# Prompt attention's query, key and value loads in another layout, and a GpSimd power for linear attention's norm root

## The chip, the cores and the metric

The kernel runs on one core of one Trainium2 chip. The metric is the device time of one execution in microseconds. A core has five engines that run side by side, each with its own in-order instruction queue: TensorE (PE in the profile, with its weight loads as a row PEld of its own), VectorE (DVE), ScalarE (ACT), GpSimd (POOL) and SyncE (SP). SP, ACT and POOL also issue DMA transfers; all of these run on the core's 16 DMA engines. SBUF has 128 partitions; PSUM takes the results of TensorE.

## The reference

One layer of a decoder, for a prompt of 2048 tokens and for 8 samples of 8 new tokens each, width 1024, all in float32:

```python
xn = rmsnorm(x, g_pre_mix)
q_a, k_a, v_a, q_b, k_b, v_b, r_b, a_lr = split(xn @ w_in)
o_a = attn_fn(q_a, k_a, v_a)             # 8 heads of 64, three dilated windows, merged
o_b = gla_recurrent(q_b, k_b, v_b, logf) # 4 heads, linear attention in chunks
o_b = rmsnorm(o_b, g_gla_norm) * silu(r_b)
x = x + rmsnorm(concat(o_a, o_b) @ w_o, g_post_mix)
x = x + rmsnorm(conv_ffn(rmsnorm(x, g_pre_ffn)), g_post_ffn)
```

The three windows of the attention, the patterns, are (128 tokens, every token), (512, every 4th) and (2048, every 16th). Each pattern has its own softmax, and the outputs are merged with weights in proportion to the softmax denominators. The norm of `o_b` is a root mean square over the 128 values of each head.

## The kernel before

The kernel has three stages. The **sweeps** (`sweeps`, line 257) go over the tokens in four chunks of 512 (the last with the 64 sample tokens as well), twice: `sweep_b` (line 650) makes the projections of linear attention, `sweep_a` (line 408) those of softmax attention. Linear attention and the sample attention are generators that are advanced between the projections, so that their work goes in between TensorE's matmuls. Then comes **prompt attention** (`attention`, line 983), then the **tail** (`tail`, line 1297) with the output projection and the feed-forward part.

Products are made in float32 as split pairs: a matrix is cut into a high part that the fast matmul format holds and the rest, and three products (high by high, high by low, low by high) are added. For the scores of softmax attention two matmuls do: the contraction runs over 128 partitions, of which 64 hold the high part of a head's queries and 64 the low part, against keys whose high part (first matmul) or low part (second) stands twice, once for each half (`at_operands`, line 1094, and line 1856).

`sweep_a` writes to scratch memory in HBM, for each of the four pairs of heads (`pr`) and each chunk c, the high and low part of the queries (tensors `qh`, `ql`, lines 445 and 446) and of the keys (`kh`, `kl`, lines 425 and 426), each [4, 128, 512]: chunk, 64 values of each of the pair's two heads, token. The values go to the output `o_vp` (line 456), a row of 512 values per token.

`attention` goes over four pairs of heads, three patterns, four groups. `at_load` (line 1062) brings a pair's queries and keys to SBUF: for each head h a tile `aqs` with the queries' two parts, a tile `akh` with the keys' high part twice, a tile `akl` with the low part twice, each [128, 2048]. Each tile is filled by two transfers (z = 0, 1) of 64 partitions. For pair 0 the load is cut into the pieces (0,1), (1,2), (2,4) of chunks, the first of them issued from ACT near the end of the sweeps (`at_prefetch`, line 965); for the others the whole of it is issued on SP while the pair before is worked on, in two sets of buffers that alternate.

`at_loadv` (line 1078) brings the values of a group in four transfers of 64 KB: four blocks of 128 keys by 128 values (two heads), each row of 512 bytes. In the first two patterns each transfer fills one block, that is a quarter of the tile's columns on all 128 partitions; in the third pattern each fills 32 partitions over all columns. The call for group i + 2 stands in the program before group i; six buffers hold them.

A unit (`AtUnit`, line 1821) is a group's scores, softmax, transposes and product with the values, for two heads; the first two patterns have two units a group, the third has one. Scores run up to three units ahead of the product. The order of the units' matmuls on TensorE is tied down (`line` in `AtUnit`), and so is the order of POOL's work (`line`, line 1114): it gathers the queries of patterns two and three into dense tiles (`at_gather`, line 1121, tile `aqg`, five buffers), and does the merge of the pair before (`at_merge`, line 1130): the weights go through HBM (line 1195) and come back spread over 64 partitions (line 1183), then multiplications and additions follow (lines 1210, 1225 and 1235). The merge advances by one step per group. For pair 3 the merge runs at the end, in another form.

The norm of linear attention's output is `gla_norm` (line 794): ACT squares and sums the four heads of a block of 128 tokens, `rms_cols` (line 100) makes one over the root, and DVE multiplies (line 803). The result is transposed on TensorE (`gla_store`, line 807). It is called 17 times: for 16 blocks of the prompt and once for the samples. `rms_cols` has two forms. With "v" the root is found on DVE, by an estimate from the bits of the number and three Newton steps: ten small instructions. With "p" it is one GpSimd instruction, a power of -0.5; the four wide norms of the layer use this one (line 132).

All else is ordered by a planner, which puts each instruction on its engine's queue in the order of a simulated timeline.

Of the kernel before, what the change touches and what calls it, by code (L numbers as in the profile page):

```python
# [10 lines left out]
F32 = mybir.dt.float32  # L11
# [25 lines left out]
class Layer:  # L37
# [370 lines left out]
    def sweep_a(self, c):  # L408
        nc, a = self.nc, self.a
        xs = self.xnext  # L410
        u = 0
        for m in range(8):
            pr, isk = m // 2, m % 2
            wt = self.wget()
            for s0, n in self.subs(c):
                ps = self.psum.tile([128, 512], F32, name=self.n("pq"), tag="g1", bufs=3)
                self.gemm([(ps[:, :n], s0, n)], wt, xs, KT)
                npr = min(n, 512 - s0)
                if s0 == 0:
                    hi = self.st.tile([128, 512], F32R, name=self.n("qh"), tag="qh", bufs=2)  # L420
                    lo = self.st.tile([128, 512], F32R, name=self.n("ql"), tag="ql", bufs=2)
                src = ps[:, :npr]
                if isk:
                    self.split(hi[:, :npr], lo[:, :npr], src, "v")
                    nc.sync.dma_start(a["kh%d" % pr][c, :, s0:s0 + npr], hi[:, :npr].bitcast(F32))
                    nc.sync.dma_start(a["kl%d" % pr][c, :, s0:s0 + npr], lo[:, :npr].bitcast(F32))
                else:
                    rr = slice(s0 // 32, (s0 + npr) // 32)
                    hv, lv = (t.rearrange("p (i r) -> p r i", r=16)[:, rr, :] for t in (hi, lo))
                    sv = src.rearrange("p (r i) -> p r i", i=32)  # L430
                    nc.scalar.activation(hv, sv, AF.Copy, scale=-0.125)
                    nc.vector.scalar_tensor_tensor(lv, sv, -0.125, hv.bitcast(F32), op0=ALU.mult, op1=ALU.subtract)
                if isk:
                    kf = self.st.tile([128, 512], F32, name=self.n("kf"), tag="kf", bufs=2)
                    self.evac(kf[:, :n], ps[:, :n], "a")
                    nc.sync.dma_start(a["o_kp"][c, pr, :, s0:s0 + npr], kf[:, :npr])
                    if npr < n:
                        nc.sync.dma_start(a["o_ks"][pr], kf[:, npr:n])
                        nc.gpsimd.tensor_copy(self.ks[:, pr, :], kf[:, npr:n])
                elif npr < n:  # L440
                    qd = self.qbd[:, pr]
                    nc.vector.tensor_copy(qd[0:64, :, 0:8], ps[0:64, npr:n].rearrange("p (b t) -> p b t", b=8))
                    nc.vector.tensor_copy(qd[64:128, :, 8:16], ps[64:128, npr:n].rearrange("p (b t) -> p b t", b=8))
            if not isk:
                nc.sync.dma_start(a["qh%d" % pr][c], hi.bitcast(F32))
                nc.sync.dma_start(a["ql%d" % pr][c], lo.bitcast(F32))
            yield "q", m
        for nn in range(2):
            wv = [self.wget(), self.wget()]
            for t0, m in self.vblocks(c):  # L450
                ps = self.psum.tile([128, 512], F32, name=self.n("pv"), tag="g1", bufs=3)
                self.vgemm(ps, xs, t0, m, wv)
                vs = self.st.tile([128, 256], F32, name=self.n("vs"), tag="vs", bufs=self.AB["vsb"])
                self.evac(vs[:m], ps[:m, :256], "v")
                if m == 128:
                    (nc.gpsimd if c == 2 else nc.sync).dma_start(a["o_vp"][c * 512 + t0:c * 512 + t0 + 128, nn * 256:nn * 256 + 256], vs)
                else:
                    nc.sync.dma_start(a["o_vs"][:, nn * 256:nn * 256 + 256], vs[:64])
                yield "v", u
                u += 1  # L460
# [333 lines left out]
    def gla_norm(self, po, n, gb):  # L794
        nc, g = self.nc, self.gp
        ss = g.tile([128, 4], F32, name=self.n("gss"), tag="gss", bufs=2)
        junk = g.tile([128, 128], F32, name=self.n("gj"), tag="gj", bufs=self.SB["gj"])
        for h in range(4):
            nc.scalar.activation(junk[:n], po[:n, h, :], AF.Square, accum_out=ss[:n, h:h + 1])
        y = self.rms_cols(ss[:n], n, 1.0 / 128, 4, g, "gr")  # L800
        on = g.tile([128, 4, 128], F32, name=self.n("gon"), tag="gon", bufs=self.SB["gon"])
        for h in range(4):
            nc.vector.scalar_tensor_tensor(on[:n, h, :], po[:n, h, :], y[:n, h:h + 1],
                                           gb[:n, h * 128:h * 128 + 128], op0=ALU.mult, op1=ALU.mult)
        return on
# [256 lines left out]
    def at_load(self, pr, pieces=((0, 4),), qs="ss", to=None):  # L1062
        a, p = self.a, self.aq[pr % 2]
        QS, KH, KL = to or ([], [], [])
        for c0, c1 in pieces:
            for h in range(2):
                hs = slice(64 * h, 64 * h + 64)
                for L, nms in ((QS, ("ql", "qh") if h else ("qh", "ql")), (KH, ("kh", "kh")), (KL, ("kl", "kl"))):
                    nm = "qs" if L is QS else nms[0]
                    if not c0:  # L1070
                        L.append(p.tile([128, 2048], F32R, name=self.n("a" + nm), tag="a" + nm, bufs=self.AB["q"]))
                    t = L[h].rearrange("p (c j) -> p c j", c=4)
                    for z in range(2):
                        self.dq(qs[z]).dma_start(t[64 * z:64 * z + 64, c0:c1].bitcast(F32),
                                                 a["%s%d" % (nms[z], pr)][c0:c1, hs].rearrange("c p j -> p c j"))
                    yield QS, KH, KL

    def at_loadv(self, i):
        nc, e = self.nc, self.nc.gpsimd if i < 2 else self.nc.sync
        pr, pat, n = i // 12, i // 4 % 3, i % 4  # L1080
        es = slice(128 * pr, 128 * pr + 128)
        vo = self.a["o_vp"]
        t = self.aq[1].tile([128, 4, 128], F32, name=self.n("av"), tag="av", bufs=self.AB["v"])
        for j in range(4):
            if pat == 0:
                e.dma_start(t[:, j, :], vo.rearrange("(c r b i) e -> c b r i e", c=4, r=16, b=4)[n, j, :, :, es])
            elif pat == 1:
                e.dma_start(t[:, j, :], vo.rearrange("(c s r i) e -> r c s i e", c=4, s=4, r=4)[n, j, :, :, es])
            else:
                e.dma_start(t[32 * j:32 * j + 32],  # L1090
                                  vo.rearrange("(c r i) e -> c i r e", c=4, r=16)[j, :, 4 * n:4 * n + 4, es])
        self.vq += [t[:, j] for j in range(4)]
# [869 lines left out]
def pack_inputs(inp):  # L1962
# [14 lines left out]
    def vt(cols):  # L1977
# [27 lines left out]
    "o_y": (128, KT, T), "o_kp": (4, 4, 128, 512), "o_vp": (S, 512), "o_gp": (2, 128, 128), "o_cp": (128, NF, 2),  # L2005
    "o_ks": (4, 128, 64), "o_vs": (64, 512), "o_gs": (2, 128, 8, 128), "o_cs": (128, NF, 8, 2),
}
SCRATCH = {**{"%s%d" % (t, i): (4, 128, 512) for t in ("qh", "ql", "kh", "kl") for i in range(4)}, "awd": (3, 96, 128),
           "wbs": (12, 2, 128, 1024), "wst": (NF // 2, 2, 4, 128, 2, 512), "xst": (4, 14, 2, 128, 2 * H),
           "mixa": (128, 4, S), "mixb": (128, 4, T), "x1": (128, KT, T), "rs1": (128, T), "rs2": (128, T)}  # L2010

# [15 lines left out]
def build(nc, arrays, stages="saf", ext_scratch=()):  # L2027
# [5 lines left out]
    with tile.TileContext(nc, **TCK) as tc:  # L2033
        with tc.tile_pool(name="scratch", bufs=1, space=bass.MemoryType.DRAM) as dp:
            for n, s in SCRATCH.items():
                if n in ext_scratch:
# [15 lines left out]
```

## Time and profile before

| | |
|---|---|
| median of 3 runs | 2780.03 us (2777.55 to 2789.05) |
| the profiled execution | 2780.57 us, its span 2778.5 us |
| mean granted TensorE clock | 0.984 |
| sweeps | 0 to about 774 us |
| prompt attention | about 774 to 1086 us |
| tail | about 1086 to 2778 us |

The profile is of one execution. Times in it are microseconds, or nanoseconds where that is said; a line such as L1856 is the line of the kernel that issued the instruction. The busy time of an engine is the sum of its instructions; matmuls are pipelined, so a busy TensorE is not TensorE at its peak. The granted clock is TensorE's, 1.00 being full speed. The DMA share is the mean busy share of the 16 DMA engines in a stretch: 0.25 is four engines' worth; it can come out a little above 1. "A <- B" says that A waited for B. In the chain of waits the work that ended last is followed back from the end, each step to what released it.

### The profile page before, as it was taken

The numbers are of one execution on the slowest core, as the hardware profiler recorded it, in microseconds if no ns is written. First come the engines' busy times: TensorE is split into PE (matmuls) and PEld (weight loads), VectorE is DVE, ScalarE is ACT, GpSimd is POOL, SyncE is SP. The second block draws the span as 40 slices with busy tenths as digits, with TensorE's granted clock in tenths as the row PEclk, the third lists the DMA queues.
The fourth block names the chain that finished last, engine by engine and source line by source line (L and its number), as shares of the span: only waits on it lengthen the run. The fifth ranks groups of instructions, "written<-read, shape, count | busy, mean of one in ns | idle before, by whom it ended". The sixth has DMA issues, their size and how long they took to land.

```text
span 2778.5 us, 58351 instructions
## 1 busy us (share of the span) xinstructions
PE 2669.0 (96%) x22203; PEld 2530.5 (91%) x22203; DVE 1827.3 (66%) x4508; ACT 1271.4 (46%) x2961; POOL 568.2 (20%) x626
## 2 busy tenths in 40 slices
PE   7999999999989898999999999999999999999998
PEld 6888899888778787999999999999999999999997
DVE  7556555454347577467898889876576766666666
ACT  6535433333358686345554444543334433443332
POOL 4424242443323577002000020000020000200001
PEclk9999999999999899999999999999999999999998
DMA  8755446799798865368587688986698875976654
GB/s 319 245 183 194 154 134 204 270 326 367 267 209 173 186 157 147 106 214 305 177 288 288 223 292 291 360 298 227 211 344 283 293 235 199 332 253 212 221 187 154
DMA packets 286183, 661.67 MB, mean 238 GB/s; under 512 B 32128, under 2 KB 81920, under 8 KB 283856
## 3 DMA queue, kind: packets, MB, share of 16 engines
q1 hardware_dynamic: 255600, 579.53, 62.0%
q0 software_dynamic: 13216, 46.56, 5.2%
q10 hardware_dynamic: 17088, 31.86, 3.1%
q8 instruction: 175, 2.87, 0.4%
q14 instruction: 104, 0.85, 0.1%
HBM read 511.45 MB, written 146.37 MB: 237 GB/s over the span
## 4 chain that ended last, share of the span: by engine, by line
PE 78%; DMA 9%; DVE 6%; POOL 2%; issue 2%; ACT 2%; SPq 0%; ACTq 0%; DVEq 0%; POOLq 0%
PE pfd L92 17%; PE pv L399 9%; PE pfe L1624 8%; PE pfd L1624 8%; PE pfa L1624 8%; PE pbo L1427 7%; PE pq L92 6%; PE pfb L1624 4%; PE pas L1856 2%; DMA av<-out_o_vp 2%; DMA ws<-d_wst 2%; PE pao L1899 1%; PE pat L1882 1%; DMA raw<-in_xp 1%; DMA akl<-d_kl 1%
## 5 line engine op out<-in xcount | busy, mean ns | idle before, releaser
L70 ACT ACTIVATE ws<-wr 128x512 fp32r<-128x512 f32 (+1 forms) x482 | 292.8, 616 | 430.9 <-PE pfe L1624 137.6
L92 PE MATMUL pfd<-hh,ws 128*128 128x264 f32 x2816 | 475.4, 286 | 8.2 <-ACT ws L70 5.5
L92 PEld LDWEIGHTS pfd<-hh,ws 128*128 128x128 f32 x2816 | 400.9, 189 | 10.6 <-ACT ws L70 7.3
L73 DVE TENSOR_TENSOR ws<-wr,ws 128x512 fp32r<-128x512 f32 (+1 forms) x482 | 319.1, 668 | 117.7 <-ACT ws L70 112.5
L92 PE MATMUL pfd<-hl,ws 128*128 128x264 f32 x1408 | 302.2, 285 | 0.0
L1624 PE MATMUL pfe<-xh,ws 128*128 128x264 f32 x1496 | 291.5, 287 | 9.5 <-DVE u L1611 5.9
L1624 PE MATMUL pfa<-xh,ws 128*128 128x264 f32 x1496 | 290.0, 285 | 4.6 <-ACT ws L70 1.9
L1624 PE MATMUL pfd<-xh,ws 128*128 128x264 f32 x1408 | 290.8, 286 | 1.8 <-DMA ws<-d_wst 1.0
L1624 PEld LDWEIGHTS pfe<-xh,ws 128*128 128x128 f32 x1496 | 237.4, 190 | 11.3 <-DVE u L1611 7.0
L1624 PEld LDWEIGHTS pfa<-xh,ws 128*128 128x128 f32 x1496 | 235.3, 188 | 5.9 <-ACT ws L70 2.4
L399 PE MATMUL pv<-wh,xh 128*128 128x256 f32 (+1 forms) x816 | 234.2, 287 | 3.2 <-DVE th L696 3.2
L1624 PEld LDWEIGHTS pfd<-xh,ws 128*128 128x128 f32 x1408 | 232.5, 190 | 2.6 <-DVE ws L73 1.4
L399 PE MATMUL pv<-wh,xl 128*128 128x256 f32 (+1 forms) x816 | 232.3, 285 | 0.0
L399 PE MATMUL pv<-wl,xh 128*128 128x256 f32 (+1 forms) x816 | 231.9, 284 | 0.0
L92 PEld LDWEIGHTS pfd<-hl,ws 128*128 128x128 f32 x1408 | 225.8, 189 | 0.1
L1865 ACT ACTIVATE ass<-ass,aml 128x256 f32<-128x256 f32 (+1 forms) x384 | 173.6, 455 | 94.5 <-DVE aml L1861 68.8
L1624 PE MATMUL pfd<-xl,ws 128*128 128x264 f32 x704 | 201.2, 286 | 0.0
L1573 POOL DMA_DIRECT2D xl<-d_xst x52 | 28.2, 542 | 834.0 <-PE pfe L1624 495.7
L92 PE MATMUL pq<-xh,wh 128*128 128x512 f32 (+2 forms) x480 | 171.3, 366 | 10.3 <-ACT xh L234 7.8
L1624 PE MATMUL pfe<-xl,ws 128*128 128x264 f32 x616 | 176.3, 286 | 0.0
L1624 PE MATMUL pfa<-xl,ws 128*128 128x264 f32 x616 | 174.9, 284 | 0.0
L92 PE MATMUL pq<-xl,wh 128*128 128x512 f32 (+2 forms) x480 | 174.8, 365 | 0.0
(338 smaller groups left out, 6569.9 us busy)
## 6 DMA issues: line engine op xcount, KB each, us to landing
ws<-d_wst SPq DMA_DIRECT2D x248, 512.0 KB
wr<-in_wu SPq DMA_DIRECT2D x114, 512.0 KB
d_wst<-ws SPq DMA_DIRECT2D x88, 512.0 KB
wr<-in_wd SPq DMA_DIRECT2D x160, 256.0 KB
wr<-in_wt SPq DMA_DIRECT2D x60, 512.0 KB
wh<-d_wbs SPq DMA_DIRECT2D x35, 512.0 KB
wl<-d_wbs SPq DMA_DIRECT2D x35, 512.0 KB
skp<-in_ckt SPq DMA_DIRECT2D x16, 1024.0 KB
```

The source lines that it names most:

```text
L70: h = nc.scalar.activation(hi, src, AF.Copy)
L73: return h, (nc.gpsimd if lo_eng == "p" else nc.vector).tensor_tensor(lo, src, hi.bitcast(F32), op=ALU.subtract)
L92: mm = nc.tensor.matmul(o, ww[:, k, :], xx[:, s0:s0 + n], start=(k == order[0] and i == 0), stop=(k == order[-1] and i == 2))
L399: mm = nc.tensor.matmul(ps[:m, :256], x[:, t0:t0 + m], w[:, k % 4, :], start=(k == 0 and i == 0), stop=(k == KT - 1 and i == 2))
L1427: self.lastmm = nc.tensor.matmul(o, ww[:, k, :], xx[:, s0:s0 + n], start=k == self.WORD[0] and i == 0, stop=k == self.WORD[-1] and i == 2)
L1573: self.nc.gpsimd.dma_start(t.bitcast(F32), xo[i, z])
L1624: self.lastmm = nc.tensor.matmul(bank[:, :H], w[:, ww, k, :], xx, start=new and k == 0 and j == 0, stop=k == 3 and j == 2, skip_group_chec ...
L1856: self.line(nc.tensor.matmul(ps[:, sc:sc + nk], lq, rk[z], start=(z == 0), stop=(z == 1)))
L1865: ex = nc.scalar.activation(ssb[:, sc:sc + nk], ssb[:, sc:sc + nk], AF.Exp, bias=self.ml[:, idx, h:h + 1], scale=-1.0, accum_out=self.ml[: ...
L1882: self.line(nc.tensor.transpose(ptp[:, len(tl), :], ssb[:, sc + 128 * j:sc + 128 * j + 128], L.ident))
L1899: self.line(nc.tensor.matmul(po[64 * h:64 * h + 64, blk, :], L.vq[self.base + kb][:, 64 * h:64 * h + 64], pt[:, j, :], start=st, stop=sp))
```

## The change

Four edits:

- The queries' two parts go into one scratch tensor `qs` of [4, 128, 2, 512] instead of two of [4, 128, 512]. Each part is still one transfer of 256 KB.
- `at_load` fills a query tile with one transfer over 128 partitions, in which the high and the low part alternate from partition to partition (both heads have the same order). It fills a key tile with one transfer per chunk, over 128 partitions, in which a step of zero makes each row of the source go to two neighbouring partitions. A pair's load of four chunks has 2 query transfers instead of 4 and 16 key transfers instead of 8. The product sums over the partitions, so that only the order of the sum changes.
- `at_loadv` loads the second pattern as it does the third: a transfer fills 32 partitions over all columns.
- `gla_norm` asks for the "p" form of `rms_cols`.

```diff
@@ sweep_a @@
             if not isk:
-                nc.sync.dma_start(a["qh%d" % pr][c], hi.bitcast(F32))
-                nc.sync.dma_start(a["ql%d" % pr][c], lo.bitcast(F32))
+                for z, t in enumerate((hi, lo)):
+                    nc.sync.dma_start(a["qs%d" % pr][c, :, z], t.bitcast(F32))
@@ gla_norm @@
-        y = self.rms_cols(ss[:n], n, 1.0 / 128, 4, g, "gr")
+        y = self.rms_cols(ss[:n], n, 1.0 / 128, 4, g, "gr", "p")
@@ at_load @@
-                for L, nms in ((QS, ("ql", "qh") if h else ("qh", "ql")), (KH, ("kh", "kh")), (KL, ("kl", "kl"))):
-                    nm = "qs" if L is QS else nms[0]
+                for L, nm in ((QS, "qs"), (KH, "kh"), (KL, "kl")):
                     if not c0:
                         L.append(p.tile([128, 2048], F32R, name=self.n("a" + nm), tag="a" + nm, bufs=self.AB["q"]))
-                    t = L[h].rearrange("p (c j) -> p c j", c=4)
-                    for z in range(2):
-                        self.dq(qs[z]).dma_start(t[64 * z:64 * z + 64, c0:c1].bitcast(F32),
-                                                 a["%s%d" % (nms[z], pr)][c0:c1, hs].rearrange("c p j -> p c j"))
+                    t = L[h].rearrange("p (c j) -> p c j", c=4).bitcast(F32)
+                    src = a["%s%d" % (nm, pr)]
+                    if L is QS:
+                        self.dq(qs[0]).dma_start(t[:, c0:c1], src[c0:c1, hs].rearrange("c p z j -> (p z) c j"))
+                    else:
+                        for c in range(c0, c1):
+                            s = src[c, hs]
+                            self.dq(qs[c % 2]).dma_start(t[:, c], bass.AP(tensor=s.tensor, offset=s.offset,
+                                                                          ap=[s.ap[0], [0, 2], s.ap[1]]))
                     yield QS, KH, KL
@@ at_loadv @@
             elif pat == 1:
-                e.dma_start(t[:, j, :], vo.rearrange("(c s r i) e -> r c s i e", c=4, s=4, r=4)[n, j, :, :, es])
+                e.dma_start(t[32 * j:32 * j + 32], vo.rearrange("(c s r i) e -> r s i c e", c=4, s=4, r=4)[n, j, :, :, es])
```

More of the change, by code (lines that the diff above doesn't have):

```diff
@@ L2007 @@
 }
-SCRATCH = {**{"%s%d" % (t, i): (4, 128, 512) for t in ("qh", "ql", "kh", "kl") for i in range(4)}, "awd": (3, 96, 128),
+SCRATCH = {**{"%s%d" % (t, i): (4, 128, 512) for t in ("kh", "kl") for i in range(4)}, **{"qs%d" % i: (4, 128, 2, 512) for i in range(4)}, "awd": (3, 96, 128),
            "wbs": (12, 2, 128, 1024), "wst": (NF // 2, 2, 4, 128, 2, 512), "xst": (4, 14, 2, 128, 2 * H),
```

## The prediction

> **What bounds the kernel now.** I read the page's first and fourth part, then the windows, the chain of waits, and the timelines of one stage.
>
> ```profile
> span 2778.5 us, 58351 instructions
> ...
> PE 2669.0 (96%) x22203; PEld 2530.5 (91%) x22203; DVE 1827.3 (66%) x4508; ACT 1271.4 (46%) x2961; POOL 568.2 (20%) x626
> ...
> PE 78%; DMA 9%; DVE 6%; POOL 2%; issue 2%; ACT 2%; SPq 0%; ACTq 0%; DVEq 0%; POOLq 0%
> ```
>
> TensorE (PE) sets the pace, so only an edit that shortens PE's gaps can pay. The windows say where these are (columns: us, then busy time of PE, PEld, DVE, ACT, POOL, granted clock, DMA share, GB/s):
>
> ```profile
> 0.00:774.00 774.00, 744.85 (x6177) 648.41 (x6177) 410.60 (x1040) 326.42 (x736) 300.04 (x297) 0.99 0.69 243
> 774.00:1086.00 312.00, 274.95 (x2632) 241.63 (x2631) 209.18 (x960) 225.60 (x872) 171.22 (x179) 0.93 0.76 172
> ```
>
> Prompt attention, 774 to 1086, loses 37 us of PE and runs at a granted clock of 0.93 on the mean. It holds most of what the change touches. The chain of waits there shows its course (start us, us, what):
>
> ```profile
> 806.15 1.16 PE pas L1856 x8
> ...
> 809.20 1.13 PE pas L1856 x8
> ...
> 844.16 1.93 PE pas L1856 x16
> ...
> 874.76 17.07 DMA av<-out_o_vp
> ...
> 893.73 15.45 DMA av<-out_o_vp
> ...
> 927.98 1.10 PE pas L1856 x8
> ...
> 943.50 17.19 DMA av<-out_o_vp
> ...
> 1004.64 1.37 PE pas L1856 x8
> ...
> 1070.47 3.67 PE pas L1856 x16
> ```
>
> Four head pairs follow each other. The first score matmul of pair 0 starts here:
>
> ```profile
> L1856 PE MATMUL pas<-akh,aqs x128: 219/287/582, 773.5 to 1028.8; 128*128 128x256 f32 x120, 128*128 128x128 f32 x8
> ```
>
> "x8" are units of the first two patterns, "x16" those of the third. An undisturbed unit takes 809.20 - 806.15 = 3.05 us; from 809.20, the first unit of the second pattern, to the last unit at 844.16 and 3.7 for that unit it is 38.7 us. Eight units of the first pattern (24.4) and these give **63 us per pair** when PE never waits. The pairs really took 773.5 to 847.9 (74.4), to 927.98 (80.1), to 1004.64 (76.7) and to 1074.15 (69.5): together 300.7. PE's gaps inside them, in its weight-load timeline:
>
> ```profile
> 793.78 0.29 PEld L1856 LDWEIGHTS pas<-akh,aqs 128*128 128x128 f32 x1 [5.31 <-issue]
> 795.19 0.28 PEld L1856 LDWEIGHTS pas<-akl,aqs 128*128 128x128 f32 x1 [1.13 <-DMA akl<-d_kl]
> ...
> 891.87 0.20 PEld L1899 LDWEIGHTS pao<-apt,av 128*64 128x64 f32 x4 [3.70 <-DMA av<-out_o_vp]
> ...
> 905.65 0.42 PEld L1899 LDWEIGHTS pao<-apt,av 128*64 128x64 f32 x8 [4.35 <-DMA av<-out_o_vp]
> 909.23 0.30 PEld L1899 LDWEIGHTS pao<-apt,av 128*64 128x64 f32 x4 [3.16 <-DMA av<-out_o_vp]
> ...
> 960.73 1.15 PEld L1899 LDWEIGHTS pao<-apt,av 128*64 128x64 f32 x12 [8.29 <-DMA av<-out_o_vp]
> ```
>
> Transfers bound this stage, in two ways that the DMA windows keep apart (us, PE busy, clock, DMA share, GB/s):
>
> ```profile
> 418.00:420.00 2.00, 2.00 (x14) 0.99 1.05 404
> 420.00:422.00 2.00, 2.00 (x19) 1.00 1.03 387
> ```
> ```profile
> 889.00:890.00 1.00, 0.00 (x0) 1.00 0.25 67
> ```
> ```profile
> 944.00:946.00 2.00, 2.00 (x20) 1.00 1.07 208
> ```
> ```profile
> 911.00:914.00 3.00, 3.00 (x16) 0.50 0.66 186
> 986.00:989.00 3.00, 3.00 (x33) 1.00 1.04 174
> ...
> 1019.00:1022.00 3.00, 3.00 (x34) 1.00 0.27 82
> ```
>
> At 944 only query and key loads run, each on 64 partitions: all 16 DMA engines are busy and move 208 GB/s. At 418 256 KB transfers over 128 partitions run, with the same 2 KB rows: as busy, they move 390 to 404. At 889 and 1019 second-pattern value loads run alone: a share of 0.25 to 0.27, four engines of 16, and 67 to 82 GB/s. In line 1088 the outermost dimension of the source has size 4; in line 1090 (third pattern) it has 32, and at 986 these loads keep all engines busy at 174 GB/s, some of it other traffic. The row at 911 shows a restart after a gap: clock 0.50, and 16 matmuls where 33 run otherwise, so that some 2 us are lost behind each longer gap.
>
> **The change part by part.** *Query and key loads.* A pair moves 12 loads (line 1074) of 64 partitions by 8 KB, 6.29 MB. At 208 GB/s that is 30.2 us of all engines, at 390 it is 16.1. Eight 512 KB key loads become sixteen of 256 KB, four query loads two of 1 MB: six more issues a pair.
>
> ```profile
> L1074 SPq DMA_DIRECT2D akh<-d_kh x20: 444/606/2774, 759.2 to 934.9; - x20
> ```
> ```profile
> L1086 SPq DMA_DIRECT2D av<-out_o_vp x56: 536/595/1096, 774.6 to 1013.1; - x56
> ```
>
> At 0.6 us an issue this adds 3.6 us to SP's queue per pair, ahead of value loads; 18 such issues and 48 value issues of at most 0.6 make 40 of some 67 us, so SP's slack hides it; without that cover it would be 4 x 3.6 = 14 us. The rate after is bounded by 208 (no gain) and 404; I take 390, because the 418 row has the same rows and number of partitions.
>
> [...]
>
> *Second-pattern value loads.* The number of partitions of one DMA falls here, from 128 (one quarter of the columns) to 32 (all columns): the words "over all 128 partitions" don't fit, what changes is the outermost dimension, 4 to 32. Sixteen loads of 64 KB a pair cost 1.05 MB / 82 GB/s = 12.8 us on four engines. Bounds after: 1.05 / 174 = 6.0 us, and no gain. I take the 174 row, since line 1090 has the very form of the new line.
>
> [...]
>
> *What is late next.* With transfers early, PE waits for POOL, which gathers queries (L1126) between the pieces of the merge of the pair before, in one fixed order:
>
> ```profile
> 1028.37 0.53 POOL L1195 DMA_DIRECT2D d_awd<-awt  x1 [14.96 <-DVE awt L65]
> ...
> 1039.15 2.99 POOL L1225 TENSOR_TENSOR aop<-aop,awb 128x512 f32<-128x512 f32 x2 [2.08 <-DMA awb<-d_awd]
> ```
> ```profile
> 887.95 2.49 POOL L1225 TENSOR_TENSOR aop<-aop,awb 128x512 f32<-128x512 f32 x2 [8.78 <-DMA awb<-d_awd]
> ```
>
> Pair 3 shows a pair with little transfer trouble: its merge starts 1039.15 - 1004.64 = 34.5 us into the pair, the last gather frees PE at 1070.47, 31.3 later, and the unit takes 3.7. In pair 1 the start came 40 us in, because the weights landed 8.78 late. With transfers early I take 34.5 - 2.1 = 32.4 for pairs 1 to 3: 32.4 + 31.3 + 3.7 = **67.4 each**, 202.2 against 226.3: **-24.0**. Bounds: 64 each (63 and the merge's matmuls), -34; and no gain.
>
> Pair 0 has no merge. It lost 74.4 - 63 = 11.4, since its 6.29 MB were still landing at 795. With 14.1 us of engine time less I leave it 4 (PE still has to fill its pipeline): **-7.4**, bounds 0 and -11.4.
>
> *Norm root of linear attention.* 17 calls lose ten DVE instructions each (one of L109, three each of L111 to L113) for one POOL power, the form that L107 has:
>
> ```profile
> L107 POOL TENSOR_TENSOR rcy<-rca,c_mhalf x17: 850/1254/2185, 26.2 to 2767.6; 128x5 f32<-128x5 f32 x12, 128x4 f32<-128x4 f32 x3, 128x3 f32<-128x3 f32 x2
> ```
> ```profile
> L111 DVE TENSOR_TENSOR grz<-gry x51: 147/162/2018, 137.8 to 504.2; 128x4 f32<-128x4 f32 x48, 64x4 f32<-64x4 f32 x3
> ```
> ```profile
> PEld pgt L811 <- DVE gon L803: 2.7, 3, 1.8
> ```
>
> About 10 x 0.163 = 1.6 us becomes 1.25 and two handovers, so a chain hardly shorter; DVE sheds some 28 us, hidden under PE. PE waited 2.7 us in all for this result. Bounds: -2.7, and the loss of rival E. I take **-1**. The writes of the queries into one tensor keep number and size, in the shadow of the projections: 0.
>
> Sum: -24.0 - 7.4 - 1 = -32.4. The profiled execution took 2780.6 (span 2778.5 and 2.1 around it), 0.5 above the median of the runs: 2748.
>
> **The rivals.** B, PE alone sets the end: pairs at 64, pair 0 without loss, -34 - 11.4 - 2.7 = -48: 2732. For it: POOL could gather earlier where the weights come early. Against: pair 3 ended on POOL. [...] E, slower: the power stands in POOL's queue behind work that waits for ScalarE, and PE, which has the transposes L811 in its order, waits with it.
>
> ```profile
> POOL wl L73 <- ACT wh L70: 161.7, 34, 17.9
> ...
> PEld pao L1899 <- DMA av<-out_o_vp: 20.0, 7, 8.3
> ```
> ```profile
> L73 POOL TENSOR_TENSOR wl<-wr,wh 128x1024 fp32r<-128x1024 f32 x48 | 119.1, 2489 | 168.7 <-ACT wh L70 161.7 <-PE pgo L942 7.0
> ```
>
> That is 4.8 us a wait, and 2.5 for the split behind it: 17 x (4.8 + 2.5 - 1.6) = +97, less 31 from attention: 2846. It decides from 31 / 17 + 1.6 = 3.4 us of queueing per power. Against it: most blocks run while POOL has small work, and the order on PE leaves a block's time before the transposes. F, no change: the merge weights stay 40 us late because they go over 64 partitions as before, and pair 0 keeps its loss: 2775.
>
> **How the numbers follow.** Forecast 0.58 (own range 2738 to 2757), B 0.10, C 0.12, D 0.10, E 0.05, F 0.05. Within 0.5% (13.9 us, about what a measurement of this kernel can tell from none) lies F and a third of C, and some of D: same 0.11; slower is E: 0.05; faster the rest, 0.84. The range 2731 to 2769 leaves out E, F, half of B and a little of C: under 2 in 10.
>
> **What would show it.** Right: windows in attention with query and key loads near 390 GB/s instead of 208; no window at a share of 0.25; waits of L1899 for `av` near zero instead of the 20.0 us of the row above; pairs of some 67 us with PE waiting for L1126; a clock above 0.93 in this stage. Wrong: a share of 1 at 208 GB/s again (C), gaps of PE before L1899 in the second pattern (D), waits of `gon` or L811 for POOL in the first 510 us (E), L1225 still starting 40 us into a pair (F).

## The result, and the profile after

The changed kernel takes 2746.11 us (median of 4 runs, 2743.86 to 2749.22), the kernel before 2778.79 beside it (median of 4, 2774.52 to 2789.05). The ratio is 0.9878, with a 95% interval of 0.9849 to 0.9907: a gain of 33 us. The forecast was 2748.0.

The first part of the page of the changed kernel, and the windows of its sweeps and of its prompt attention (columns as in the prediction: us, busy time of PE, PEld, DVE, ACT, POOL, granted clock, DMA share, GB/s):

```profile
span 2745.3 us, 58213 instructions
...
PE 2655.9 (97%) x22203; PEld 2520.9 (92%) x22203; DVE 1791.5 (65%) x4338; ACT 1270.2 (46%) x2961; POOL 587.2 (21%) x643
```
```profile
0.00:774.00 774.00, 747.27 (x6204) 652.23 (x6204) 378.13 (x891) 328.61 (x749) 318.46 (x318) 0.99 0.70 246
774.00:1056.00 282.00, 264.59 (x2623) 234.12 (x2622) 208.45 (x946) 223.81 (x863) 171.97 (x181) 0.97 0.64 184
```

Attention's clock went from 0.93 to 0.97 and its DMA share from 0.76 to 0.64, though the same bytes are moved. Windows with one row for each head pair, the kernel before and then the changed one, from the first score matmul of a pair to that of the next:

```profile
773.34:847.95 74.61, 62.92 (x590) 55.69 (x588) 43.78 (x215) 53.11 (x208) 22.88 (x25) 0.91 0.84 183
847.95:927.91 79.96, 69.49 (x661) 61.28 (x660) 51.58 (x242) 55.62 (x218) 44.45 (x45) 0.91 0.82 176
927.91:1004.57 76.66, 67.59 (x661) 59.22 (x660) 51.65 (x242) 57.26 (x224) 45.72 (x47) 0.94 0.83 186
1004.57:1073.96 69.39, 64.84 (x638) 57.32 (x636) 54.47 (x237) 55.52 (x209) 49.12 (x48) 0.97 0.62 156
```
```profile
769.92:831.22 61.30, 58.47 (x589) 51.81 (x587) 43.30 (x215) 52.78 (x208) 23.06 (x25) 1.00 0.76 247
831.22:900.77 69.55, 67.09 (x662) 59.75 (x660) 51.27 (x242) 57.10 (x224) 42.51 (x43) 0.95 0.66 182
900.77:972.42 71.65, 67.20 (x661) 59.77 (x660) 51.50 (x242) 55.88 (x217) 49.23 (x50) 0.95 0.66 191
972.42:1037.72 65.30, 62.89 (x638) 55.78 (x636) 54.13 (x237) 55.17 (x209) 46.01 (x47) 0.99 0.60 156
```

The four pairs fell from 300.6 to 267.8 us (-32.8). Attention begins 3.4 us earlier (769.92 instead of 773.34), and what follows the last pair became 3.1 us longer (2745.3 - 1037.72 = 1707.6, before 2778.5 - 1073.96 = 1704.5). These add up to the span's 33.2. PE's waits in attention, from the list of waits (us in total, times, longest), before and after:

```profile
PEld pao L1899 <- DMA av<-out_o_vp: 20.0, 7, 8.3
...
PEld pas L1856 <- POOL aqg L1126: 5.5, 6, 3.0
```
```profile
PEld pas L1860 <- POOL aqg L1130: 10.8, 10, 3.0
...
PEld pas L1860 <- DMA akl<-d_kl: 1.1, 1, 1.1
...
PEld pao L1903 <- DMA av<-out_o_vp: 0.8, 5, 0.2
```

The lines behind `at_load` carry numbers 4 higher now. The wait for the values is gone, and the wait for POOL's gathers has doubled: POOL is what is late next. Two DMA windows with query and key loads; in the first, transfers of POOL's queue take 0.45 of the share beside them, in the second they run alone:

```profile
762.00:768.00 6.00, 6.00 (x53) 6.00 (x52) 1.04 (x3) 0.00 (x0) 1.09 (x2) 1.00 1.05 392
...
792.00:798.00 6.00, 6.00 (x64) 5.49 (x61) 4.05 (x18) 5.39 (x21) 1.68 (x2) 1.00 1.05 389
```

All engines are busy as before, and move 389 to 392 GB/s instead of 208.

### The profile page after: what moved, and what is told of

Same layout as the page of the kernel before. It is cut to its first block, busy times and chain, and to the rows that moved or that the text cites. A ratio compares the mean times of both kernels' runs of the same rounds, so it can differ in the third digit from the quotient of the medians.

```text
span 2745.3 us, 58213 instructions
## 1 busy us (share of the span) xinstructions
PE 2655.9 (97%) x22203; PEld 2520.9 (92%) x22203; DVE 1791.5 (65%) x4338; ACT 1270.2 (46%) x2961; POOL 587.2 (21%) x643
## 5 line engine op out<-in xcount | busy, mean ns | idle before, releaser
L1869 ACT ACTIVATE ass<-ass,aml 128x256 f32<-128x256 f32 (+1 forms) x384 | 173.5, 454 | 63.7 <-DVE aml L1865 37.9
L92 PE MATMUL pq<-xh,wh 128*128 128x512 f32 (+2 forms) x480 | 170.9, 364 | 10.7 <-ACT xh L234 7.9
```

What stands on the lines that cost most here:

```text
L92: mm = nc.tensor.matmul(o, ww[:, k, :], xx[:, s0:s0 + n], start=(k == order[0] and i == 0), stop=(k == order[-1] and i == 2))
L1869: ex = nc.scalar.activation(ssb[:, sc:sc + nk], ssb[:, sc:sc + nk], AF.Exp, bias=self.ml[:, idx, h:h + 1], scale=-1.0, accum_out=self.ml[: ...
```

## The experiments

Two theories stood at the start. Mine: query and key loads were slow because each went to one half of the partitions, second-pattern value loads because they ran on four engines; with both gone, POOL's row of gathers and merge sets the end of pairs 1 to 3. The rivals: the gain comes from one of the edits alone (or from the norm), and POOL's waits are a symptom. All runs, with the start of pair 0, the four pairs by the same windows, and the rest behind them, from the profiles. The last three columns are of one profiled execution each, which lies up to 7.4 us from the median (2775.07 for the value loads alone, 2765.6 for the merge a step earlier), so differences of a few us between them are not certain:

| kernel | us (median) | ratio to before, 95% | pair 0 starts | pairs 0 to 3 | rest |
|---|---|---|---|---|---|
| before | 2778.8 to 2782.5 | | 773.3 | 74.6, 80.0, 76.7, 69.4 | 1704.5 |
| changed | 2746.11 | 0.9878 (0.9849 to 0.9907) | 769.9 | 61.3, 69.5, 71.6, 65.3 | 1707.6 |
| query and key layout alone | 2770.27 | 0.9961 (0.9948 to 0.9974) | 775.7 | 62.9, 74.6, 74.9, 68.5 | 1712.3 |
| value loads alone | 2768.86 | 0.9962 (0.9948 to 0.9976) | 771.8 | 76.0, 77.4, 73.0, 67.5 | 1707.7 |
| norm power alone | 2779.04 | 1.0 (0.9988 to 1.0013) | 767.2 | 75.8, 76.9, 77.7, 69.3 | 1709.6 |
| changed without the power | 2750.33 | 0.9889 (0.9872 to 0.9905) | 773.3 | 62.4, 69.0, 71.1, 66.3 | 1706.3 |
| changed, L1214 on DVE | 2745.8 | 0.9879 (0.9863 to 0.9896) | 767.2 | 62.5, 68.8, 71.3, 68.8 | 1705.1 |
| changed, stores on SP | 2735.32 | 0.9836 (0.982 to 0.9852) | 769.5 | 63.8, 66.1, 71.0, 63.4 | 1698.2 |
| stores and weights on SP | 2726.42 | 0.9804 (0.9789 to 0.9819) | 766.6 | 62.0, 64.1, 68.1, 62.9 | 1701.5 |
| the same, value loads as before | 2739.97 | 0.9856 (0.9841 to 0.9871) | 765.5 | 61.7, 66.5, 74.3, 62.9 | 1702.9 |
| changed, merge a step earlier | 2758.2 | 0.9918 (0.9904 to 0.9933) | 769.6 | 61.6, 76.5, 74.4, 72.2 | 1709.4 |
| changed, keys to even and odd | 2754.55 | 0.9906 (0.9891 to 0.9922) | 767.9 | 72.6, 68.5, 69.7, 66.4 | 1709.9 |
| before, halves on two queues | 2807.15 | 1.0084 (1.0066 to 1.0103) | 772.7 | 94.1, 84.4, 81.4, 69.8 | 1704.3 |

**The edits one by one.** First the query and key layout (the kernel before with that part of the diff alone):

```diff
-                    for z in range(2):
-                        self.dq(qs[z]).dma_start(t[64 * z:64 * z + 64, c0:c1].bitcast(F32),
...
+                        self.dq(qs[0]).dma_start(t[:, c0:c1], src[c0:c1, hs].rearrange("c p z j -> (p z) c j"))
...
+                            self.dq(qs[c % 2]).dma_start(t[:, c], bass.AP(tensor=s.tensor, offset=s.offset,
...
```

> The kernel before with the query and key layout alone (one scratch tensor for the queries, loads over 128 partitions); second-pattern value loads and the norm root as before. My theory: the loads themselves were the cost, so pair 0 falls from 74.6 to about 61 to 62 us as in the changed kernel (-13), the query and key windows show about 390 GB/s, and the value loads, which no longer queue behind 30 us of them, cause little of their 20.0 us of waits (half is left, some 10 with the slow restarts): -25, about 2754. Rival 1: the value loads on four engines are a limit of their own, all 20 us of waits stay: -13, about 2766. Rival 2: the value loads were late only because of what stood before them: no waits for av are left, -30, about 2749.

Pair 0 did what my theory said (62.9). In pairs 1 to 3 rival 2 named the right wait: PE's wait for `av` in attention is 0.7 us, without any edit of the value loads. Yet pairs 1 and 2 stay 5.1 and 3.3 us longer than in the changed kernel. The attention gained 19.7 us; the whole gained only 10.4, since the sweeps and the rest were together 10 us longer in this profile. So the total lies above all three forecasts, and why the 10 us outside attention were lost is not known. Then the value loads alone:

```diff
-                e.dma_start(t[:, j, :], vo.rearrange("(c s r i) e -> r c s i e", c=4, s=4, r=4)[n, j, :, :, es])
+                e.dma_start(t[32 * j:32 * j + 32], vo.rearrange("(c s r i) e -> r s i c e", c=4, s=4, r=4)[n, j, :, :, es])
```

> The kernel before with the second-pattern value loads in the new form alone. My theory: the loads land in half the time, but still wait on SP's queue and the engines behind query and key loads that hold all engines for 30 us a pair: some of the 20.0 us of PE's waits for av go, -10, about 2768; pair 0 stays at 74 to 75 us. Rival 1: four engines were the whole cause of the waits: they go to near 0, pairs 1 to 3 fall by 20 together, 2758. Rival 2: no gain at all without the other edit, 2778.

-11.8 us on the whole, where I expected -10: my theory by the total. Its profile shows -6.8 in attention, and PE's wait for `av` falls from 20.0 to 5.5 us. Pair 0 keeps its loss. The power alone:

```diff
-        y = self.rms_cols(ss[:n], n, 1.0 / 128, 4, g, "gr")
+        y = self.rms_cols(ss[:n], n, 1.0 / 128, 4, g, "gr", "p")
```

> The kernel before with the GpSimd power in linear attention's norm alone. My theory, from the changed kernel's sweeps, which end at 769.8 us instead of 773.2: the whole 3.4 us come from the power, attention stays at about 300.7 us for its four pairs, 2775. Rival 1: the 3.4 us come from the writes and prefetched loads of the new query layout, the power gives 0 to -1: 2778. Rival 2: work that DVE no longer does lets the planner order attention otherwise, and more than 5 us move.

The sweeps end 6.1 us earlier (767.2), but the rest is 5.1 longer and the whole the same: rival 1 by the total, and neither by the place. The opposite cut, the changed kernel with the norm root on DVE:

```diff
-        y = self.rms_cols(ss[:n], n, 1.0 / 128, 4, g, "gr", "p")
+        y = self.rms_cols(ss[:n], n, 1.0 / 128, 4, g, "gr")
```

> The changed kernel with the norm root on DVE as before, so that it has the query, key and value loads alone. My theory: the two layouts together give what they don't give one by one (10.8 and 10.6 us alone), since the one's gain is held up by the other's transfers; the power shortens the sweeps by some 5 us in the profiles (they end at 766.5 to 769.8 us with it, 771.7 to 775.6 without) and the whole by 0 to 5: 2748. Rival: the missing 13 us come from the power, which together with them gives what it didn't give alone: 2759.

2750.33: the two layouts together give nearly the whole gain, and the power is not the missing 13 us. In attention the layouts give 31.8 us together and 19.7 + 6.8 = 26.5 one by one. The difference is no larger than the spread: the profile with 6.8 is of the slowest of six executions, 6 us above their median. That the two need each other is therefore not shown by these sums.

**What slow value loads do besides.** The kernel with the query and key layout alone and the changed kernel without the power differ in the value loads only. POOL's timeline of pair 1 in the one and the other (start us, us, what, and in brackets the idle time before it and what ended it):

```profile
866.19 1.05 POOL L1187 DMA_DIRECT2D awb<-d_awd  x2 [2.47 <-DMA d_awd<-awt]
...
876.27 1.27 POOL L1229 TENSOR_TENSOR aop<-aop,awb 128x512 f32<-128x512 f32 x1 [5.87 <-DMA awb<-d_awd]
```
```profile
862.93 1.05 POOL L1187 DMA_DIRECT2D awb<-d_awd  x2 [2.03 <-DMA d_awd<-awt]
...
869.11 1.27 POOL L1229 TENSOR_TENSOR aop<-aop,awb 128x512 f32<-128x512 f32 x1 [2.00 <-DMA awb<-d_awd]
```

By DMA queue, the transfers from the issue of the weights to the first multiplication in the one and in the other (packets, MB, share of the 16 engines; q0 is POOL's and carries the weights, q1 is SP's):

```profile
q0 software_dynamic: 284, 1.40, 60.5%
q1 hardware_dynamic: 905, 0.90, 35.9%
```
```profile
q0 software_dynamic: 218, 1.14, 82.4%
q1 hardware_dynamic: 123, 0.05, 3.0%
```

From the issue of the merge's weights to the first multiplication 10.1 us pass in the one and 6.2 in the other. In the one SP's queue holds 0.36 of the engines in that time, in the other 0.03: first loads of `akl`, issued from 861.94 on (in the other the last was issued at 857.94), then value loads. The merge starts 37.7, 37.9 and 34.1 us into pairs 1 to 3, against 33.4, 34.1 and 32.6, and the pairs are 5.6, 3.8 and 2.2 longer, about what the start is late; PE's waits for the gathers are 18.6 us against 9.6. So value loads on four engines (a share of 0.27 at 82 GB/s in the kernel before, the row at 1019) cost through the merge's weights, not only through PE's own wait: by these rows through engines that they hold themselves and through key loads that come later on SP's queue; how much each costs is not shown. I tested that on the fastest kernel (below), with the value loads' old form put back:

```diff
-                e.dma_start(t[32 * j:32 * j + 32], vo.rearrange("(c s r i) e -> r s i c e", c=4, s=4, r=4)[n, j, :, :, es])
+                e.dma_start(t[:, j, :], vo.rearrange("(c s r i) e -> r c s i e", c=4, s=4, r=4)[n, j, :, :, es])
```

> The kernel with the merge's stores and weight loads on SP, with the second-pattern value loads as in the kernel before (outermost dimension 4, four engines). My theory: such loads cost more than their own waits, because the merge's weights pass through the same engines; the weights land later, as in the run with the query and key layout alone (10.1 us behind the issue instead of 5.9), so that the merge starts some 3 to 5 us later in each of pairs 1 to 3, and each ends so much later: +8 to +13 against 2726, 2736. Rival 1: with work taken off POOL there is slack for it, and PE waits nowhere: 2728. Rival 2: SP stands for the weights now, and slow values come late for PE itself: waits for av of 10 us or more, 2745.

POOL's timeline of pair 2, at the first multiplication of the merge:

```profile
936.57 2.50 POOL L1229 TENSOR_TENSOR aop<-aop,awb 128x512 f32<-128x512 f32 x2 [11.67 <-DMA awb<-d_awd]
```

+13.6 us, of which 8.3 in attention. In pair 2, where POOL stands 11.67 us for the weights, the merge starts 6.4 us later and the pair is 6.2 longer; in pair 1 it is 3.4 and 2.4; in pair 3 the start and the length stay. That is my theory, with more than it said in pair 2 and nothing in pair 3. In this kernel the weights stand in SP's queue right behind four of the slow loads (the first is issued at 926.11), and from 926.6 to 928.7 the DMA share is only 0.2 to 0.3.

**POOL as the next bound.** Take work off POOL, first one addition:

```diff
-                    line(nc.gpsimd.tensor_tensor(OP[1][:, :, sl], OP[1][:, :, sl], OP[0][:, :, sl], op=ALU.add))
+                    nc.vector.tensor_tensor(OP[1][:, :, sl], OP[1][:, :, sl], OP[0][:, :, sl], op=ALU.add)
```

> The changed kernel with one of the merge's steps, the addition of line 1214 (1.30 us on POOL, four a pair, pairs 0 to 2), on DVE, where such an addition took 0.69. My theory: POOL's row of gathers and merge is the bound in pairs 1 to 3; four additions less shorten it by 5.2 us a pair, PE's 10 waits for the gathers (10.8 us, and slow restarts behind them) go mostly, and these pairs fall from 206.5 toward 3 x 64 = 192: -10 against the changed kernel, about 2736. Rival 1: the multiplication after the addition now waits for DVE, which is busy with the softmax, as long as the addition took: 0, 2746. Rival 2: DVE, busy for 208 of 282 us in this stage, becomes late with its own work, some 3 us a pair: 2755.

A row of POOL's timeline of this kernel, and two of the view of the tile `aop` (ns, min/median/max, first and last start):

```profile
884.15 1.29 POOL L1239 TENSOR_TENSOR amo<-aop,aop 128x512 f32<-128x512 f32 x1 [3.56 <-DVE aop L1214]
```
```profile
L1214 DVE TENSOR_TENSOR aop<-aop,aop x12: 679/1680/2575, 868.1 to 1043.9; 128x512 f32<-128x512 f32 x12
...
L1237 DVE TENSOR_TENSOR aop<-aop,aop x4: 678/699/1141, 1056.3 to 1065.7; 128x512 f32<-128x512 f32 x4
```

No gain: rival 1. POOL's timeline shows it standing for DVE, which has the softmax in its queue first (10.7 us in four waits). And the view of the tile shows that the addition is slow there: 1680 ns in the median, against 699 for the same shape in L1237 at the end. In the trace the four of the twelve that no POOL instruction overlapped took 679 to 683 ns, the eight others 1209 to 2575. Why the overlap costs so much is not shown.

So the next two runs take work off POOL that waits on nothing new: the merge's stores, and then its weight loads too, go to SP.

```diff
-            line(nc.gpsimd.dma_start(self.a["mixa"][:, pr, 512 * cb:512 * cb + 512], mo))
+            if last:
+                line(nc.gpsimd.dma_start(self.a["mixa"][:, pr, 512 * cb:512 * cb + 512], mo))
+            else:
+                nc.sync.dma_start(self.a["mixa"][:, pr, 512 * cb:512 * cb + 512], mo)
```

> The changed kernel with the merge's stores (line 1241, 0.61 us to issue and 0.30 of waiting ahead of it, four a pair, pairs 0 to 2) on SP's queue instead of POOL's. The addition of the run with line 1214 on DVE failed because POOL stood for DVE (3.56 us at one place), so this takes work off POOL without a new wait on it. My theory: POOL's row from the merge's start to the last gather is what ends pairs 1 to 3; three stores before the last gather, 2.7 us a pair, come off: 206.5 to about 199, 2738. Rival 1: SP waits for POOL at each store, value loads behind it come late, and PE waits for them instead: 2746 or more. Rival 2: the restarts after a gap, which stay, hold the time: 2744.

```diff
-                    line(nc.gpsimd.dma_start(W[64 * h:64 * h + 64],
+                    nc.sync.dma_start(W[64 * h:64 * h + 64],
...
```

> The same with the loads of the merge's weights (line 1187, 0.52 us each, eight a pair) on SP as well. My theory: another 3 to 4 us a pair come off POOL's row, PE's 10.8 us of waits for the gathers go nearly to zero, the clock in attention rises over 0.98, pairs 1 to 3 reach about 64 each: 2732. Rival 1: SP stands for the weights' way through HBM (4.3 us from store to load, and the buffers that POOL frees), the values queued behind it come late: 2750. Rival 2: as for the stores alone, nothing more: same time as that run.

Pair 1 of the second in the windows by pair, and PE's wait for the gathers in its list of waits:

```profile
828.66:892.75 64.09, 64.07 (x661) 56.96 (x659) 51.24 (x242) 55.41 (x218) 35.45 (x32) 1.00 0.70 188
```
```profile
PEld pas L1863 <- POOL aqg L1130: 4.1, 7, 2.0
```

2735.32 and 2726.42: the waits for the gathers fall from 10.8 over 6.1 to 4.1 us, pairs 1 to 3 from 206.5 over 200.4 to 195.0 (expected were some 199 and 192). That is the direction and nearly the size of my theory. The totals fell by more: the second kernel beats the changed one by 20 us, of which only 10.7 lie in the four pairs of the profiles, 3.3 ahead of them and 6.1 behind; in the first 3.6 lie in the pairs and 9.4 behind. What was gained outside attention is not explained, so that the agreement of the totals is in part luck. In pair 1 of the second PE is busy for 64.07 of 64.09 us.

Its weight loads themselves stay slow. A window in which they run alone:

```profile
926.00:930.00 4.00, 4.00 (x42) 3.49 (x43) 3.08 (x16) 3.43 (x13) 0.73 (x1) 1.00 1.01 217
```

All engines are busy at 217 GB/s. Each of these loads fills 64 neighbouring partitions, one half, as the query and key loads did before (L1187); no run here changes that.

The last run on POOL makes the first multiplication follow the weights' issue by one group less:

```diff
-    AB = dict(mw=1, qg=5, ...
+    AB = dict(mw=0, qg=5, ...
```

> The changed kernel with the merge's first multiplication one step (a group) earlier in POOL's order, right behind the issue of the weights' loads. My theory: pairs end a fixed time after the merge starts, so that they follow its start: with weights landing 5.4 us after their issue the start moves by some 1 us in pair 1 and 3 in pairs 2 and 3, -6, 2740. Rival 1: POOL now stands for the weights with gathers behind it, and PE waits earlier in the pair: +5, 2751. Rival 2: start and end of the merge don't set the pairs at all: 2746.

POOL's timeline of this kernel in pair 1, and PE's wait for the gathers in its list of waits:

```profile
858.00 2.05 POOL L1187 DMA_DIRECT2D awb<-d_awd  x4 [1.62 <-DMA d_awd<-awt]
864.05 2.51 POOL L1229 TENSOR_TENSOR aop<-aop,awb 128x512 f32<-128x512 f32 x2 [4.00 <-DMA awb<-d_awd]
866.64 1.29 POOL L1214 TENSOR_TENSOR aop<-aop,aop 128x512 f32<-128x512 f32 x1
867.87 2.19 POOL L1130 CAST aqg<-aqs 128x512 fp32r<-128x512 f32 x2
```
```profile
PEld pas L1860 <- POOL aqg L1130: 19.6, 19, 3.2
```

+12 us against the changed kernel: rival 1, at more than twice its price, and I was wrong. The merge starts where it did (32.8, 34.9 and 32.0 us in), because the weights land no earlier; POOL stands 4.00 us for them with a gather behind it, and each later gather stands behind one more piece of the merge. PE's waits for the gathers rise to 19.6 us in 19 places. What decides is how much of POOL's row lies ahead of a gather, not the merge's start alone.

**Why 208 GB/s.** Two runs keep transfers of 64 partitions. In the first, on the changed kernel, a key tile is filled by two transfers of 512 KB, one for even and one for odd partitions:

```diff
-                        for c in range(c0, c1):
-                            s = src[c, hs]
-                            self.dq(qs[c % 2]).dma_start(t[:, c], bass.AP(tensor=s.tensor, offset=s.offset,
-                                                                          ap=[s.ap[0], [0, 2], s.ap[1]]))
+                        tz = t.rearrange("(p z) c j -> z p c j", z=2)
+                        for z in range(2):
+                            self.dq(qs[0]).dma_start(tz[z, :, c0:c1], src[c0:c1, hs].rearrange("c p j -> p c j"))
```

> The changed kernel with its key tiles filled by two transfers of 64 partitions and 512 KB, as in the kernel before, but one for the even and one for the odd partitions instead of one for each half; the row of each key still goes to the same two partitions. My theory: what held the loads before at 208 GB/s was that each transfer wrote into one half of the partitions; spread over both halves the same number of partitions moves about 390 GB/s, pair 0 stays at 61 to 63 us and the whole at 2746. Rival 1: 64 partitions a transfer are the limit, 208 GB/s again for keys (4.2 MB of 6.3), and pair 0 about 70 us, the whole at 2760. Rival 2: what helps in the changed kernel is that one read serves two partitions, or the smaller transfers: the rate falls to 208 here as well.

Two windows of this kernel, then SP's timeline and PE's at the start of pair 0:

```profile
789.00:792.00 3.00, 3.00 (x36) 2.66 (x34) 2.17 (x10) 2.67 (x11) 0.00 (x0) 1.00 1.05 395
795.00:798.00 3.00, 3.00 (x36) 2.66 (x34) 1.55 (x9) 2.90 (x12) 0.00 (x0) 1.00 1.05 385
```
```profile
769.09 1.29 SPq L1078 DMA_DIRECT2D akh<-d_kh  x2
770.43 1.26 SPq L1078 DMA_DIRECT2D akl<-d_kl  x2
...
772.37 1.26 SPq L1078 DMA_DIRECT2D akh<-d_kh  x2
773.67 1.26 SPq L1078 DMA_DIRECT2D akl<-d_kl  x2
```
```profile
775.13 0.55 PE L1859 MATMUL pas<-akh,aqs 128*128 128x256 f32 x1 [6.78 <-DMA akh<-d_kh]
776.76 0.55 PE L1859 MATMUL pas<-akl,aqs 128*128 128x256 f32 x1 [1.07 <-DMA akl<-d_kl]
...
779.76 0.55 PE L1859 MATMUL pas<-akh,aqs 128*128 128x256 f32 x1 [2.13 <-DMA akh<-d_kh]
781.30 0.58 PE L1859 MATMUL pas<-akl,aqs 128*128 128x256 f32 x1 [0.99 <-DMA akl<-d_kl]
```

The rate is my theory's: 385 to 395 GB/s with 64 partitions a transfer, 512 KB each and one row read for one partition. Where these loads differ from those at 208 GB/s is that the partitions of each lie in both halves. The time of pair 0 is not my theory's: 72.6. SP's timeline and PE's show why. PE stands four times in the first unit, 11.0 us in all, and they end 6 to 8 us behind the issues on SP of the loads for the last two chunks of the pair's four key tiles, in the same order. The trace's semaphores name these loads: the later of the first two landed at 775.00, and PE started at 775.13. The first unit reads the first chunk only. So it seems that with a step in the partitions the program takes these loads for something that the unit reads and makes it wait; why it does is not shown. Without the 11.0 us pair 0 would take 61.6 by this estimate, as in the changed kernel, and pairs 1 to 3 (204.6) are like its own. The second run takes the kernel before and issues the loads of the upper half on ACT:

```diff
-    def at_load(self, pr, pieces=((0, 4),), qs="ss", to=None):
+    def at_load(self, pr, pieces=((0, 4),), qs="sa", to=None):
```

> The kernel before with one change of its own: of the two transfers of 64 partitions that fill a query or key tile, the one for partitions 64 to 127 is issued on ACT's queue instead of SP's, so that loads of the lower and the upper half run at the same time; sizes, rows and sources stay. My theory: the 208 GB/s came from all engines writing into one half of the partitions at a time; with both halves at once the rate rises toward 390 GB/s, and pair 0 falls from 74.6 to about 63 us. Rival: the rate belongs to a transfer of 64 partitions by 8 KB as such, whatever runs beside it: 208 GB/s and 74 to 76 us again. The time of the whole says little, since six issues a pair on ACT (0.6 us each) stand among the exponentials: anything from 2750 to 2785.

Windows of this kernel in which pair 1 is loaded:

```profile
804.00:806.00 2.00, 1.55 (x9) 1.31 (x7) 1.77 (x9) 0.04 (x1) 0.00 (x0) 0.69 1.10 202
808.00:810.00 2.00, 0.00 (x0) 0.00 (x0) 0.00 (x0) 0.00 (x0) 0.00 (x0) 0.67 1.05 226
812.00:814.00 2.00, 2.00 (x17) 1.67 (x16) 0.20 (x1) 0.00 (x0) 0.00 (x0) 0.50 1.06 369
818.00:820.00 2.00, 1.32 (x8) 0.99 (x10) 0.00 (x0) 2.00 (x9) 0.00 (x0) 0.73 1.05 363
```

From 810 to 822 both queues move data and the rate is 345 to 374 GB/s; from 804 to 810 both do as well, at 200 to 226. In part the two queues take turns in the first 6 us: from 805 to 807.5 ACT's has 0.82 of the engines and SP's 0.24, from 807.5 to 809 SP's has 0.83 and ACT's 0.22, while from 810 on each has 0.52 to 0.53. But from 809 to 810 each has 0.53 too, at 225 GB/s, so the rest stays open. The six windows of the later 12 us move 363 GB/s on the mean, 74% above the 208; the three of the earlier six 209, no gain. The kernel as a whole is slower, 2807.15, outside what I allowed: PE waited 20.2 us for ACT's copies (L63), which stand in one queue with the issues, and pair 0 took 94.1.

## Why the prediction was right, and where it was off

The total was right within 2 us, in part by luck, since its errors nearly cancelled: in the profiles pair 0 gained 13.3 (forecast 7.4), pairs 1 to 3 gained 19.5 (24.0), the sweeps 3.4 (1), and what follows lost 3.1 (0).

*What bounds the kernel.* Right: nearly all of the gain lies in prompt attention, and it is PE's waits and slow clock that went: PE's matmuls are as many, 22203.

*Query and key loads.* Right: 390 GB/s was taken, 389 measured where they run alone. To put the 208 GB/s down to 64 partitions as such was too wide: 64 partitions of one half moved 208, 64 spread over both halves 385 to 395. The size of a transfer did not decide: key loads of 256 KB (389) and of 512 KB (385 to 395) ran at the same rate. That SP's slack hides six more issues held: PE waited 1.1 us for `akl` in all of attention.

*Second-pattern value loads.* Right that the new form is faster, though not by as much as taken. A window of the changed kernel in which such loads run alone:

```profile
784.00:786.00 2.00, 2.00 (x25) 1.83 (x25) 1.53 (x9) 1.46 (x5) 0.00 (x0) 1.00 0.48 139
```

139 GB/s stand against 82 in the row at 1019, and against the 174 that I took. SP issued eight of these loads in 3.91 us, which makes 134 GB/s, so by this estimate SP's pace set the rate and not the engines. The row at 889 was misread: there the merge's weights have 0.17 of the engines and the values 0.05, and only the row at 1019 shows the values alone. Nor was a window at a share of 0.25 a good sign: third-pattern loads show 0.20 in the changed kernel, from 868 to 874. Most of PE's wait for `av` needed both old layouts: 20.0 us with both, 5.5 with the new value loads alone, 0.7 with the new query and key loads alone, 0.8 with both new. So slow value loads alone did not bring the sign put down for D, gaps of PE before L1899; the merge's weights came late instead (10.1 us behind their issue against 6.2).

*What is late next.* Right in kind. The start of the merge was forecast 32.4 us into each pair and came at 32.7, 34.8 and 32.0. From there to the pair's end I took pair 3's 35.0; it was 36.9, 36.8 and 33.3. POOL's part of that was as taken: the gather that frees PE's last unit came 30.1, 30.0 and 30.9 us behind the merge's start (taken: 31.3). Too small was the piece behind it in pairs 1 and 2, 6.8 us instead of 3.7: PE restarts there at a mean granted clock of 0.54, while in pair 0, where no gap stands before the last unit, the same piece took 3.9 us at 1.00. The sum was 206.5 instead of 202.2, so the term of -24.0 was -19.5. The windows at the end of pair 1 show POOL full and, behind PE's gap, six microseconds at half the clock:

```profile
891.00:894.00 3.00, 0.55 (x11) 0.31 (x7) 0.98 (x2) 2.21 (x11) 2.92 (x4) 0.90 0.61 135
894.00:897.00 3.00, 3.00 (x14) 3.00 (x15) 0.91 (x8) 0.57 (x3) 2.92 (x3) 0.50 0.51 107
897.00:900.00 3.00, 3.00 (x18) 2.67 (x19) 1.56 (x11) 2.94 (x15) 2.68 (x4) 0.50 1.06 368
```

*Pair 0.* The term of -7.4 was -13.3, beyond its bound of -11.4. The step that was mis-sized is the floor of 63 us for every pair. Pair 0 begins without products of a pair before: 589 matmuls lie in it, 661 in pair 1, and PE is busy for 58.47 us. Against that floor PE lost 61.3 - 58.5 = 2.8, near the 4 that I left it.

*Norm root.* -1 was forecast, bounded by -2.7. Pair 0 starts at 765.5 to 769.9 us in the eight profiles with the power and at 771.8 to 775.7 in the five without: about 5 us, beyond the bound, which counted only PE's waits for `gon`. Of the total no run tells it from nothing (1.0, 0.9988 to 1.0013, alone; 0.9878 against 0.9889 in the changed kernel, the intervals overlap). Where the sweeps' 5 us go then is not settled: the rest behind attention varies from 1698.2 to 1712.3 us between these kernels, whose code there is the same, though the planner orders it a little otherwise in each. Rival E did not happen: DVE waited 9.9 us for the power, PE 1.2 for `gon`.

*The writes of the queries*: nothing seen, as forecast. *Rivals C and D*: neither sign was seen in the changed kernel (for C a share of 1 at 208 GB/s again, for D gaps of PE before L1899): query and key loads ran at 389 GB/s, and PE waited 0.8 us for `av`. The single edits came to 2768.86 (value loads, expected at 2768) and 2770.27 (queries and keys, expected at 2754). In the second, attention gained 19.7 us of the 25, with the late merge shown above (in pairs 1 to 3), and 10 us were lost outside attention, which no run explains.

## What to carry to other kernels

Judge a transfer by which partitions it writes (here 208 to 217 GB/s for one half, 385 to 395 for both) and by its outermost dimension (82 GB/s with 4, 139 with 32, for loads of 64 KB), not by its number of partitions alone or, at the 256 KB to 1 MB seen here, by its size. Look for traffic that shares its queue and its engines: here slow value loads made the merge's weights late, and the pairs with them. Price the restart behind a gap with the gap: the piece behind it took 6.8 us at a mean granted clock of 0.54, and 3.9 at 1.00 without a gap. When a wait is removed, look for the next queue with a written order: here it was POOL's. DMA issues, moved to SP, left that queue without waiting on another busy engine and gave what moving arithmetic to DVE did not (2726.42 against 2745.8). Look where a gain lies before you credit it: about half of the gain of the fastest kernel over the changed one lies outside the stage that was edited. Give each pass of a loop its own floor: the first lacks the work that is carried over.

## What was not expected of the hardware

- Transfers of 64 partitions ran at 385 to 395 GB/s when they were spread over both halves (keys to even and odd), and at 208 (query and key loads of the kernel before) or 217 (the merge's weights) when they filled one half.
- An addition of 128x512 on DVE took 1209 to 2575 ns where POOL's gathers and multiplications overlapped it, and 679 to 683 ns where nothing of POOL did.
- The longest issues were longer where transfers were slow. In the view of the tile `av` (ns, min/median/max) one issue of a second-pattern value load took up to 6901 ns before and 1443 after:

```profile
L1088 SPq DMA_DIRECT2D av<-out_o_vp x64: 528/564/6901, 792.5 to 1032.2; - x64
```
```profile
L1092 SPq DMA_DIRECT2D av<-out_o_vp x64: 311/430/1443, 782.0 to 998.9; - x64
```

With either layout alone the longest took 2077 (keys and queries) and 1688 (values).
